# A hybrid decoder step on one core: TensorE in the traced order, the other engines placed by the scheduler

## The chip, the cores and the metric

The kernel runs on one core of one Trainium2 chip. A core has five engines that each work through their own instruction queue: TensorE (PE in the profile, its weight loads shown apart as PEld), VectorE (DVE), ScalarE (ACT), GpSimd (POOL) and SyncE (SP), which here issues the DMAs. The metric is the device time of one execution in microseconds. Before the change the median of three runs was 3425.92 us (3423.82 to 3428.62). A change of under 0.2% (7 us) counts as no difference in what follows.

## What is computed

One layer of a decoder for a prompt of 2048 tokens and for 8 sequences with 8 new tokens each, which have a past of 2048 tokens in pages of keys and values. The reference, cut to what matters:

```python
h = rmsnorm(x, norm_mix) * (1 + sc_m) + sh_m            # sh, sc, g: silu(c) @ w_ada + b_ada
rq, rk, rv, rg, sq, sk, sv = jnp.split(h @ w_in, cuts, axis=-1)
# 4 heads of retention, in chunks of 128 tokens with a running state s
scores = einsum(qc, kc) * decay
o = einsum(scores, vc) + einsum(qc * q_decay, s); s = s * chunk_decay + einsum(kc * k_decay, vc)
ro = groupnorm(o) * ret_gn * silu(rg)
# 8 heads of stick-breaking attention; k, v are the past pages and the new rows
z = q @ k * scale + bias
a = exp(log_sigmoid(z) + reverse_cumsum(log_sigmoid(-z)))    # only keys before the query
so = rmsnorm_per_head(a @ v) * sb_gn
x = x + g_m * (concat([ro, so]) @ w_out)
h = rmsnorm(x, norm_ffn) * (1 + sc_f) + sh_f
x = x + g_f * ((silu(conv3(h @ w_up_gate)) * (h @ w_up_val)) @ w_down)
y = rmsnorm(x, norm_final)
```

## The kernel before

All of it is float32. A dense product is made as three products of values split in a high and a low part: `mm3` (L293) issues them as L295, L296 and L297, so that every weight tile has to be split first, by a cast on ACT (L174) and a subtraction on DVE (L159, the helper through which most tensor operations go). The weight parts are the tiles `whl`, from raw weights `raw` that SP loads; the activations are `act` and `ff`.

The prompt is worked on in four blocks of 512 tokens. The work is written as Python generators, each of which records some instructions and yields a cost: `in_block` (adaLN, input projections; `k_rows` L640 transposes the new keys at L643), `decode` (the 8 sequences against their pages), `ada`, `retention` and `retention_sample`, `attention`, and `mlps` (`out_block` and `ffn_block` for each block of tokens). `_weave` (L138) steps them in turn: it takes the generator whose cost so far is the smallest share of its given total. The order in which the instructions are recorded in this way is the **traced order**. There are three weaves: `in_block`, `decode` and `ada`; then the rest of `in_block` and `ada` with both retentions and the attention of block 0; then `mlps` with the attention of blocks 1 to 3. The last `ffn_block` stands alone.

Three pieces of it matter below, since the change moves them:

- **Attention** (L1122) makes one step for each 128 queries by 512 keys: `turn` of five steps ago (transposes the attention weights, L1173, into a PSUM tile `z`, which ACT and DVE split into the two tiles `ahl`), then `av` of six steps ago (L1185, two matmuls a split, `acc <- ahl, avv`), then `qk` (L1144, two matmuls into a `z`, which ACT turns into `aom` and `abe` at L1147 and L1148, then a scan on DVE). So `av` uses what the `turn` of the step before gave to ACT and DVE.
- **Decode** (L775) makes for each pair of key pages: `k_load` (transposes at L835, which ACT and DVE split into `khl`) and, in the next step, `k_z` (L848, reads `khl`); for the value pages `v_load` (ACT and DVE split the page into `vhl`) and, a step later, `v_mm` (L908, `acc <- vhl, aT`). Pages are loaded into 3 buffers (`page`), `vhl` has 3 buffers, `khl` 2.
- **PSUM** has 4 buffers `d`, 3 buffers `z` and one `acc`; a `z` is free for the next use when ACT or DVE has read it.

After the trace a **scheduler** decides in which order each engine's queue holds its instructions. It plays the program through with estimated durations. Whenever an engine is free in that play, it gets the first instruction in traced order whose inputs and buffers are ready by these estimates; one that isn't ready is passed by. The five queues are then fixed, with the waits on semaphores between them.

## Time and profile before

| | |
|---|---|
| median of 3 runs | 3425.92 us |
| the profiled execution | 3422.1 us |
| its span (first to last instruction) | 3420.4 us |
| mean granted TensorE clock | 0.986 |
| busy DVE, ACT, POOL | 2287.6, 1772.8, 1029.1 us |
| DMA | 527.72 MB, mean 154 GB/s |

A matmul row of the profile has its engine, line, operation, the tiles it writes and reads, the sizes, and its duration; matmuls overlap one another, so a run of 512-column matmuls that the page shows with a mean of 367 to 408 ns each starts one about every 230 ns. "Idle before" is time in which the engine did nothing before an instruction, with the instruction that ended the wait.

### The profile page before, as it was taken

The page shows a single profiled execution, that of the slowest core. Times are in us where ns is not written, and L with a number is a line of the kernel's source. Part 1 is how long each engine was busy: PE and PEld are TensorE (multiplying, and loading weights), DVE is VectorE, ACT ScalarE, POOL GpSimd, SP SyncE. Part 2 cuts the span into 40 slices and gives each one's busy share as a digit, 9 for nine tenths or more (in the row PEclk, how much of TensorE's full clock was granted, in tenths as well). Part 3 has the DMA queues.
Part 4 walks back from the last instruction along what each step waited for, and adds up shares of the span by engine and source line. Part 5 has one row for each costly group of instructions (what it writes and reads, how often), then busy time and mean ns, then how long its engine had stood idle before and what let it go on. Part 6 is the DMA issues. An engine that isn't in the chain of part 4 may idle for free.

```text
span 3420.4 us, 49521 instructions
## 1 busy us (share of the span) xinstructions
PE 3273.5 (96%) x17111; PEld 2676.8 (78%) x17111; DVE 2287.6 (67%) x3258; ACT 1772.8 (52%) x3153; POOL 1029.1 (30%) x1898
## 2 busy tenths in 40 slices
PE   7999999999988989999998999999899999899998
PEld 5877777776777768878877877877788787799997
DVE  5466666764665567777778777877878774554445
ACT  5457556654544446555556555555655553433223
POOL 3012001101443233433344343334433333221113
PEclk9999999999999999999999999999999999999999
DMA  6765776776656773433464343336333334332221
GB/s 235 234 202 191 235 235 209 239 241 206 198 179 193 243 224 95 126 117 113 123 199 122 117 120 108 118 113 197 118 115 108 114 105 146 106 109 81 81 87 66
DMA packets 406233, 527.72 MB, mean 154 GB/s; under 512 B 27830, under 2 KB 244009, under 8 KB 405982
## 3 DMA queue, kind: packets, MB, share of 16 engines
q1 hardware_dynamic: 405982, 524.55, 49.0%
q8 instruction: 136, 2.23, 0.3%
q14 instruction: 115, 0.94, 0.1%
HBM read 442.47 MB, written 81.99 MB: 153 GB/s over the span
## 4 chain that ended last, share of the span: by engine, by line
PE 45%; DVE 2%; POOL 1%; ACT 1%; issue 1%; DMA 1%; SPq 0%; POOLq 0%; DVEq 0%; ACTq 0%
PE d L295 11%; PE d L296 11%; PE d L297 11%; PE acc L1185 3%; PE z L1144 2%; PE z L1173 2%; PE z L297 1%; PE z L296 1%; PE z L295 1%; DVE whl L159 1%; DVE hf L159 1%; DVE aom L1161 0%; POOL ff L159 0%; ACT whl L174 0%; PE z L304 0%
## 5 line engine op out<-in xcount | busy, mean ns | idle before, releaser
L174 ACT CAST whl<-raw 128x1024 fp32r<-128x1024 f32 x456 | 477.2, 1050 | 940.9 <-PE d L296 661.7
L159 DVE TENSOR_TENSOR whl<-raw,whl 128x1024 fp32r<-128x1024 f32 x456 | 573.9, 1262 | 523.1 <-ACT whl L174 514.2
L295 PE MATMUL d<-act,whl 128*128 128x512 f32 (+2 forms) x2016 | 738.8, 367 | 2.3 <-DVE hf L159 1.4
L297 PE MATMUL d<-act,whl 128*128 128x512 f32 (+2 forms) x2016 | 734.3, 364 | 1.1 <-DVE whl L159 1.1
L296 PE MATMUL d<-act,whl 128*128 128x512 f32 (+2 forms) x2016 | 730.9, 363 | 0.2
L295 PEld LDWEIGHTS d<-act,whl 128*128 128x128 f32 x2016 | 382.7, 190 | 62.4 <-issue 3.1
L297 PEld LDWEIGHTS d<-act,whl 128*128 128x128 f32 x2016 | 382.1, 190 | 60.6 <-DVE whl L159 2.2
L296 PEld LDWEIGHTS d<-act,whl 128*128 128x128 f32 x2016 | 383.5, 190 | 55.9 <-issue 0.4
L295 PE MATMUL d<-whl,ff 128*128 128x512 f32 x704 | 279.3, 397 | 0.0
L296 PE MATMUL d<-whl,ff 128*128 128x512 f32 x704 | 278.9, 396 | 0.0
L297 PE MATMUL d<-whl,ff 128*128 128x512 f32 x704 | 278.3, 395 | 0.0
L295 PE MATMUL d<-whl,act 128*128 128x512 f32 x640 | 257.5, 408 | 5.5 <-ACT whl L174 5.5
L296 PE MATMUL d<-whl,act 128*128 128x512 f32 x640 | 258.8, 404 | 0.3 <-DVE whl L159 0.3
L1161 DVE TENSOR_TENSOR_SCAN aom<-aom,acy 128x512 f32<-128x512 f32 x192 | 256.0, 1333 | 3.1 <-ACT aom L1147 2.4
L297 PE MATMUL d<-whl,act 128*128 128x512 f32 x640 | 257.3, 403 | 0.0
L159 DVE TENSOR_TENSOR abe<-abe,aom 128x512 f32<-128x512 f32 (+2 forms) x320 | 230.1, 719 | 29.9 <-POOL abe L1151 7.9
L1185 PE MATMUL acc<-ahl,avv 128*128 128x512 f32 (+3 forms) x640 | 223.5, 411 | 18.4 <-DVE ahl L159 8.4
L1147 ACT ACTIVATE aom<-z,nb 128x512 f32<-128x512 f32 (+2 forms) x320 | 200.9, 628 | 72.6 <-PE z L1144 50.0
L1148 ACT ACTIVATE abe<-z,bb 128x512 f32<-128x512 f32 (+2 forms) x320 | 199.6, 624 | 0.0
L1144 PE MATMUL z<-akk,aq 128*128 128x512 f32 (+3 forms) x640 | 190.5, 375 | 8.6 <-DVE scd L159 5.9
L159 DVE TENSOR_TENSOR ahl<-z,ahl 128x512 fp32r<-128x512 f32 (+1 forms) x320 | 191.3, 598 | 10.3 <-ACT ahl L174 9.9
L1343 DVE SCALAR_TENSOR_TENSOR c<-a,vecs,c 128x512 f32<-128x512 f32 x176 | 133.3, 759 | 81.8 <-ACT c L1340 47.2
(295 smaller groups left out, 6238.9 us busy)
## 6 DMA issues: line engine op xcount, KB each, us to landing
raw<-in_w_in SPq DMA_DIRECT2D x56, 1024.0 KB
raw<-in_w_up_gate SPq DMA_DIRECT2D x44, 1024.0 KB
raw<-in_w_up_val SPq DMA_DIRECT2D x44, 1024.0 KB
akk<-k SPq DMA_DIRECT2D x160, 256.0 KB
page<-in_cache_k_pages SPq DMA_DIRECT2D x128, 256.0 KB
page<-in_cache_v_pages SPq DMA_DIRECT2D x128, 256.0 KB
raw<-in_w_down SPq DMA_DIRECT2D x32, 1024.0 KB
raw<-in_w_ada SPq DMA_DIRECT2D x24, 1024.0 KB
```

The lines of the kernel that those rows point to most:

```text
L159: eng.tensor_tensor(o, a, b, op)
L174: act.copy(hi, src)
L295: pe.matmul(ps, sh, mh, start=start, stop=False)
L296: pe.matmul(ps, sh, ml, start=False, stop=False)
L297: pe.matmul(ps, sl, mh, start=False, stop=stop)
L1144: pe.matmul(z[:, :n], qs[g, h][:, i * P : (i + 1) * P], kk[:, c, :n], start=c == 0, stop=c == 1)
L1147: act.activation(om[:, :n], z[:, :n], AF.Sigmoid, bias=nb[:, h : h + 1], scale=-SCALE)
L1148: act.activation(be[:, :n], z[:, :n], AF.Sigmoid, bias=bb[:, h : h + 1], scale=SCALE)
L1161: dve.tensor_tensor_scan(rv, rv, rv, init, ALU.mult, ALU.bypass)
L1173: pe.transpose(ps[:, i * P : (i + 1) * P], As[u, i][:, kt * P : (kt + 1) * P], ident)
L1185: pe.matmul(accs[0][:, cs], kv[u][1][:, kt, :], m[:, cs], start=(s == g and kt == 0 and c == 0), stop=(s == 0 and kt == NT - 1 and c == 1),)
L1343: dve.scalar_tensor_tensor(c[:, :TB], a[:, j : j + TB], cw(j), c[:, :TB], ALU.mult, ALU.add)
```

## The change

The whole recording now stands in a context that tells the scheduler to leave TensorE's queue as it was traced:

```diff
     with _tile.TileContext(nc) as tc:
-        body(tc, ins, outs)
+        with tc.manual_schedule(engines={mybir.EngineType.PE}):
+            body(tc, ins, outs)
```

No instruction is added or removed. TensorE has 16,670 matmuls and transposes in both. The scheduler still places those of DVE, ACT, POOL and SP, in a play in which TensorE waits at its next instruction in traced order instead of passing it by. Set side by side, the two TensorE queues are equal but for 172 separate stretches, at whose ends the same instructions have been issued; they hold 4,355 instructions. Of the other queues 777 of 3,258 instructions stand elsewhere on DVE, 840 of 3,050 on ACT, 209 of 1,898 on POOL, and 757 of 1,617 on SP; on DVE and ACT by at most 35 places.

The first place is on TensorE, where `decode` begins to compute (185 us into the profiled execution). L835 are transposes of a key page, L848 the scores of `k_z`, L529 a piece of `ada`, L295 to L297 with `d_435` the first projection of the next `in_block` chunk. The queue before:

```order
L835 MATMUL z_407_1939<-con_106_171,page_406_1937 128x128 x4
L295 MATMUL d_435_2081<-act0_114_193,whl_433_2077 128x288
L296 MATMUL d_435_2081<-act0_114_193,whl_433_2077 128x288
L297 MATMUL d_435_2081<-act0_114_193,whl_434_2078 128x288
L295 MATMUL d_435_2081<-act0_114_193,whl_433_2077 128x288
L296 MATMUL d_435_2081<-act0_114_193,whl_433_2077 128x288
L297 MATMUL d_435_2081<-act0_114_193,whl_434_2078 128x288
L848 MATMUL z_408_1946<-khl_403_1907,qbd_402_1901 128x264
```

The queue of the change at the same place (the last number of a name is two higher throughout):

```order
L835 MATMUL z_407_1941<-con_106_173,page_406_1939 128x128 x4
L848 MATMUL z_408_1948<-khl_403_1909,qbd_402_1903 128x264 x8
L835 MATMUL z_415_1983<-con_106_173,page_414_1981 128x128 x4
L835 MATMUL z_417_2001<-con_106_173,page_416_1999 128x128 x4
L529 MATMUL z_420_2011<-whl_421_2012,s18_120_228 18x512
```

The scores `z_408` follow the transposes before them at once; the projection, of which six matmuls stood between them, comes only after two more steps of `decode` and the piece of `ada`.

The second place is on TensorE beside the MLP (1511 us), where two steps of `attention` follow each other without a piece of `mlps` between. `acc_3443` is the attention's output, `ahl_3509` and `ahl_3510` the two halves of one split, `z_3520` the next scores, and `d_3524` to `d_3526` the down projection. The queue before:

```order
L1173 MATMUL z_3516_17903<-con_106_171,abe_3501_17831 128x128
L1185 MATMUL acc_3443_17551<-ahl_3509_17882,avv_3423_17471 128x512
L295 MATMUL d_3524_17929<-whl_3529_17935,ff_3366_17211 128x512
L296 MATMUL d_3524_17929<-whl_3530_17936,ff_3366_17211 128x512
L297 MATMUL d_3524_17929<-whl_3529_17935,ff_3366_17211 128x512
L295 MATMUL d_3525_17930<-whl_3529_17935,ff_3366_17211 128x512
L296 MATMUL d_3525_17930<-whl_3530_17936,ff_3366_17211 128x512
L1144 MATMUL z_3520_17917<-akk_3511_17888,aq_3466_17665 128x512
L1185 MATMUL acc_3443_17551<-ahl_3510_17883,avv_3423_17471 128x512
L1144 MATMUL z_3520_17917<-akk_3511_17888,aq_3466_17665 128x512
```

The queue of the change at the same place:

```order
L1173 MATMUL z_3516_17905<-con_106_173,abe_3501_17833 128x128
L1185 MATMUL acc_3443_17553<-ahl_3509_17884,avv_3423_17473 128x512
L1185 MATMUL acc_3443_17553<-ahl_3510_17885,avv_3423_17473 128x512
L1144 MATMUL z_3520_17919<-akk_3511_17890,aq_3466_17667 128x512 x2
L295 MATMUL d_3524_17931<-whl_3529_17937,ff_3366_17213 128x512
L296 MATMUL d_3524_17931<-whl_3530_17938,ff_3366_17213 128x512
```

The second matmul of `av` and both of `qk` now stand ahead of the five matmuls of the down projection that stood before them.

## The prediction

> **What bounds the kernel now.** I read the page first, then the busy time of each engine by stage.

> ```profile
> span 3420.4 us, 49521 instructions
> PE 3273.5 (96%) x17111; PEld 2676.8 (78%) x17111; DVE 2287.6 (67%) x3258; ACT 1772.8 (52%) x3153; POOL 1029.1 (30%) x1898
> ```

> ```profile
> core 0: us, PE busy (x) PEld busy (x) DVE busy (x) ACT busy (x) POOL busy (x), PEclk, DMA share, GB/s
> 0.00:185.00 185.00, 162.78 (x986) 130.14 (x987) 93.59 (x124) 93.61 (x157) 38.08 (x68) 0.96 0.70 235
> 185.00:815.00 630.00, 602.66 (x3234) 479.00 (x3234) 411.09 (x626) 381.03 (x695) 83.13 (x171) 0.99 0.68 220
> 815.00:1293.00 478.00, 430.85 (x2311) 345.85 (x2312) 280.35 (x578) 224.64 (x458) 176.86 (x372) 0.97 0.66 203
> 1293.00:2870.00 1577.00, 1552.49 (x7414) 1247.35 (x7414) 1230.01 (x1525) 877.16 (x1490) 610.06 (x1040) 1.00 0.41 123
> 2870.00:3421.00 551.00, 524.75 (x3169) 474.46 (x3168) 272.58 (x406) 196.32 (x357) 120.97 (x247) 0.97 0.31 99
> ```

> TensorE is the bound in every stage: 3273.5 of 3420.4 us, idle for 147 us in all. In the longest stage, attention beside the MLP, it is idle for 24 of 1577 us, and no other engine passes 78% there (DVE, 1230 of 1577). So a microsecond in which TensorE stands still is a microsecond of the end, and the change can only move the time by making it wait more or less.

> **The change part by part.** It adds and removes nothing. TensorE's queue differs in 172 stretches. In each, the queue of before passes by an instruction and does other work first; that of the change stops at it. What this costs is read from the trace: when TensorE came to the place, and when ACT, DVE, POOL or a DMA had ended what the passed instruction needs. At the first place that the change section shows:

> ```profile
> 185.29 0.38 PE L295 MATMUL d<-act,whl 128*128 128x288 f32 x1
> 186.44 0.42 DVE L159 TENSOR_TENSOR z<-z,zl 64x264 f32<-64x264 f32 x1
> 186.79 1.27 DVE L159 TENSOR_TENSOR khl<-z,khl 128x512 fp32r<-128x512 f32 x2
> ```

> TensorE was there at 185.29. The scores that now come next need a `z` that DVE reads until 186.86 and the last low half of `khl`, which ends at 188.06. So it would stand for 1.6 us, issue one matmul and stand again for about 1 us. The longest wait of this stage is at a value page:

> ```profile
> 287.60 1.12 PE L848 MATMUL z<-khl,qbd 128*128 128x256 f32 x8
> 293.01 0.60 ACT L174 CAST vhl<-page 128x512 fp32r<-128x512 f32 x1
> ```

> The change has `v_mm` (L908) at 287.60; its cast ends at 293.61, 6 us later. The last place of the stage is small:

> ```profile
> 806.33 0.69 DVE L159 TENSOR_TENSOR vhl<-page,vhl 128x512 fp32r<-128x512 f32 x1 [2.23 <-ACT vhl L174]
> 806.69 0.39 PE L295 MATMUL d<-act,whl 128*128 128x512 f32 x1
> ```

> Its first `v_mm` would start at 807.02 instead of 806.69; with those behind it this place costs 2.9 us.

> I did this for every stretch: its matmuls in the new order, each at the spacing that it has in the trace, none before its inputs' end as traced; what the stretch ends later is its cost. The stage from 185 to 815 has 50 stretches, from the one at 185.29 to that at 806.69, and they cost **106 us**; 60 us of waits are of `v_mm` for a value page.

> Beside the MLP there are 79 stretches, from 1302.88 to 2839.17. The first, the second place of the change section, and the last:

> ```profile
> 1302.88 0.48 PE L295 MATMUL d<-act,whl 128*128 128x512 f32 x1
> 1306.55 0.67 DVE L159 TENSOR_TENSOR o<-acc,sbsq 64x512 f32<-64x512 f32 x1
> ...
> 1511.82 0.39 PE L295 MATMUL d<-whl,ff 128*128 128x512 f32 x1
> 1512.58 0.68 DVE L159 TENSOR_TENSOR ahl<-z,ahl 128x512 fp32r<-128x512 f32 x1
> 1513.36 0.46 PE L1185 MATMUL acc<-ahl,avv 128*128 128x512 f32 x1
> ...
> 2839.17 0.48 PE L295 MATMUL d<-act,whl 128*128 128x512 f32 x1
> 2840.79 0.68 DVE L159 TENSOR_TENSOR ahl<-z,ahl 128x512 fp32r<-128x512 f32 x1
> ```

> At 1302.88 `av` would wait for DVE to read the old `acc` until 1307.22, 4.3 us. At 1511.82 it would wait until 1513.26 for the low half of the split, 1.4 us, while the down projection stands behind it. At 2839.17 the low half ends at 2841.47, 2.3 us. In 64 of the 79 the longest wait is one of `av`; they recur because two attention steps come without a piece of the MLP between. The 79 cost **130 us**.

> The three other stages have one place each here:

> ```profile
> 87.15 0.38 PE L295 MATMUL d<-act,whl 128*128 128x288 f32 x1
> 88.01 0.40 ACT L634 COPY kf<-z 128x288 f32<-128x288 f32 x1
> ...
> 925.93 0.50 PE L295 MATMUL d<-act,whl 128*128 128x512 f32 x1
> 926.23 0.68 ACT L1148 ACTIVATE abe<-z,bb 128x512 f32<-128x512 f32 x1
> ...
> 2956.98 0.40 PE L295 MATMUL d<-whl,ff 128*128 128x512 f32 x1
> 2960.28 1.33 ACT L1293 ACTIVATE c<-ff,rs_b 128x512 f32<-128x512 f32 x2
> ```

> The key transposes wait for a copy that ends at 88.41, 1.3 us; 12 stretches before 185 cost 11 us. The retention's scores wait for ACT to free a `z` at 926.91, 1.0 us; 27 stretches from 815 to 1293 cost 67 us, the long chains of the norms among them. The transposes before the last block's MLP wait for the first of two ACT copies (2960.28 + 0.67), 4 us; four stretches after 2870 cost 7 us. Sum: 11 + 106 + 67 + 130 + 7 = **321 us**.

> What stands behind a waiting matmul is all of TensorE's queue, and behind that, with the same delay, whatever ACT and DVE make of it. Both bounds of the sum lie there. **Above:** I held the producers to their traced times, though most of them start from a TensorE instruction that itself comes later. Timing every producer from the one that feeds it, with the lag that it has in the trace, gives 385 us. **Below:** while TensorE stands, ACT and DVE work off what they have. With nothing queued ahead, the split at 1511.82 is a cast and a subtraction (0.58 and 0.68) after the transposes, against 0.6 of `qk` on TensorE: 0.7 us instead of 1.4. Half the sum, 160 us. I take 321: beside the MLP the queues of DVE and ACT read the same at most of these places before and after, so the same work is queued ahead.

> **The clock** is a second term. Three neighbouring windows of 3.4 us, with TensorE's busy time, its granted clock, the DMA share and GB/s:

> ```profile
> 2419.50:2422.90 3.40, 1.18 (x6) 1.00 0.80 253
> 2422.90:2426.30 3.40, 3.40 (x19) 0.50 0.27 67
> 2426.30:2429.70 3.40, 3.40 (x30) 1.00 0.40 155
> ```

> After a window with TensorE busy for 1.18 us the clock is granted at half for the next, with 19 matmuls instead of 30. So an added wait of some 2 us can halve the next 3.4 us and cost up to 1.7 more. My list holds 59 waits of over 1.9 us; if half of them fall whole within such a window, that is 29 x 1.7 = 50 us at most. Nothing is the other end, since TensorE may be waiting then anyway. I take 30 us, nearer to the row's full price.

> [...]

> Against the profiled execution: 3422.1 + 321 + 30 = 3773. The median of the runs shown is 3.8 us above that execution, so **3777 us**.

> **The rivals.** *The waits melt away.* ACT and DVE, idle for 48% and 33% of the span, get ahead in each wait and the next is shorter. For it speaks the lower bound above; against it that the waits are some 20 us apart beside the MLP, far more than the queue of a wait. It gives 3426 + 160 = 3586.

> *The waits breed.* Chains repeat and the clock falls at most of them: 3426 + 385 + 50 = 3861 and more.

> *Faster.* The queue of before was laid by estimates, and TensorE waits in it, too (us in total, times, longest):

> ```profile
> PE z L835 <- DMA page<-in_cache_k_pages: 5.8, 8, 1.6
> PE z L835 <- issue: 3.1, 1, 3.1
> PE acc L908 <- ACT vhl L174: 6.2, 9, 2.0
> PE acc L908 <- DVE vhl L159: 2.1, 6, 0.7
> PE acc L1185 <- DVE ahl L159: 8.4, 11, 2.3
> PE acc L1185 <- ACT ahl L174: 6.7, 5, 2.5
> ```

> Where a passed instruction was ready on the chip already, or one was pulled ahead and then waited, the traced order loses nothing. By my count 84 us of the idle time lie within the 172 stretches. If they vanished and the new waits came to less than 84 us, the kernel would gain, with half of them left some 42 us: 3384. It decides where the new waits are a quarter of my sum. Against it: 154 of the 172 stretches cost over 0.3 us by the traced times, so the instruction passed by was late on the chip, too.

> *It does nothing*, since other work hides it or the orders come out alike: 3426. The rows of the change section and TensorE's 96% are against it. Nor does a matmul pass a waiting one by itself:

> ```profile
> 1513.03 0.19 PEld L1144 LDWEIGHTS z<-akk,aq 128*128 128x128 f32 x1 [0.32 <-ACT abe L1148]
> 1513.89 0.39 PE L297 MATMUL d<-whl,ff 128*128 128x512 f32 x1
> ```

> L1144 waited for 0.32 us; L297, whose like had been running just before, stood behind it until 1513.89.

> **How the numbers follow.** Forecast, as worked out, 0.75 (its own range 3680 to 3860); melting 0.11 (3480 to 3680); breeding 0.09 (3860 to 4000); faster 0.03; no difference 0.02, where within 0.2% (7 us) is what a measurement cannot tell from no change. The range of 8 in 10 takes the forecast's and the nearer part of melting and breeding: **3600 to 3880**. Faster 0.03, same 0.02, slower 0.95.

> **What would show it.** TensorE's busy time should stay near 3270 while its idle time rises from 147 to some 470 us (the clock adds busy time); the waits of L1185 for `ahl` should grow from some 15 to over 100 us, those of L908 for `vhl` from 8 to some 60; DVE and ACT should keep their busy time. More entries of half clock should appear from 185 to 1293. The prediction is wrong if L1185 does not lead the list of waits, if idle time grows by less than 160 us, or if DVE or ACT near saturation take over the bound.

## The result, and the profile after

| | before | after |
|---|---|---|
| median | 3426.23 us (4 runs) | 3782.63 us (3779.06 to 3783.46, 4 runs) |
| ratio | | 1.1026, 95% interval 1.1012 to 1.104 |
| TensorE idle (span less busy) | 146.9 us | 398.0 us |
| time at half clock | 98.4 us in 17 stretches | 365.4 us in 64 stretches |

Half clock is the time for which the profile shows a granted TensorE clock of 0.5. The changed kernel is 10% slower: 356 us where 351 were forecast. Three of its four executions have a mean granted clock of 0.952 to 0.954; the fourth shows 0.907 although it is the shortest (3779.06 us), and why stays open. The page's head and TensorE's busy time, after:

```profile
span 3781.8 us, 49606 instructions
PE 3383.8 (89%) x17111; PEld 2776.6 (73%) x17111; DVE 2296.9 (61%) x3258; ACT 1777.7 (47%) x3153; POOL 1019.1 (27%) x1898
```

DVE and ACT have worked as long as before (2287.6 and 1772.8 us). TensorE idles for 251 us more, and the same instructions keep it busy for 110 us longer. The busy time by stage of the kernel after, cut where the same TensorE instructions stand as at the stage bounds of the prediction:

```profile
core 0: us, PE busy (x) PEld busy (x) DVE busy (x) ACT busy (x) POOL busy (x), PEclk, DMA share, GB/s
0.00:200.50 200.50, 169.30 (x987) 136.51 (x988) 94.24 (x124) 94.12 (x157) 40.29 (x68) 0.93 0.66 218
200.50:956.80 756.30, 647.26 (x3233) 514.95 (x3233) 418.92 (x631) 385.12 (x699) 85.89 (x171) 0.93 0.58 189
956.80:1505.50 548.70, 450.76 (x2314) 369.13 (x2313) 285.35 (x577) 227.05 (x460) 175.89 (x373) 0.90 0.55 169
1505.50:3224.00 1718.50, 1590.80 (x7415) 1279.91 (x7414) 1227.23 (x1521) 875.20 (x1482) 592.12 (x1039) 0.98 0.38 113
3224.00:3781.80 557.80, 525.63 (x3169) 476.13 (x3167) 271.16 (x406) 196.21 (x357) 124.90 (x247) 0.97 0.30 98
```

Set against the same rows of before (span, and span less TensorE's busy time):

| stage (bounds of before) | waits forecast | longer by | of it idle | of it busy |
|---|---|---|---|---|
| 0 to 185 | 11 | 15.5 | 9.0 | 6.5 |
| 185 to 815, decode | 106 | 126.3 | 81.7 | 44.6 |
| 815 to 1293 | 67 | 70.7 | 50.8 | 19.9 |
| 1293 to 2870, beside the MLP | 130 | 141.5 | 103.2 | 38.3 |
| 2870 to the end | 7 | 7.4 | 6.5 | 0.9 |
| sum | 321 | 361 | 251 | 110 |

The granted clock (PEclk) has fallen in every stage but the last, most from 185 to 1293: from 0.99 and 0.97 to 0.93 and 0.90. TensorE's longest waits after (us in total, times, longest):

```profile
PE acc L1185 <- DVE ahl L159: 58.8, 62, 2.0
PE acc L1185 <- ACT ahl L174: 22.9, 20, 4.6
PE acc L908 <- ACT vhl L174: 19.8, 11, 4.3
PE acc L1185 <- DVE o L159: 18.3, 6, 4.1
PE d L295 <- DVE hf L159: 14.0, 3, 6.4
PE acc L908 <- DVE vhl L159: 13.9, 13, 2.6
PE z L835 <- DVE z L159: 13.8, 13, 3.0
PE z L1144 <- DVE scd L159: 13.7, 8, 2.6
PE z L1144 <- DMA akk<-k: 13.5, 1, 13.5
```

L1185 leads, with 81.7 us for `ahl` (15.1 before); L908 waits for `vhl` for 33.7 us (8.3 before). Three of the places worked out in the prediction, in the timeline after: the first scores of decode (185.29 of before), the first `av` of the third weave (1302.88), and the down projection (1511.82):

```profile
202.43 0.36 PE L848 MATMUL z<-khl,qbd 128*128 128x264 f32 x1 [1.47 <-DVE z L159]
203.63 1.88 PE L848 MATMUL z<-khl,qbd 128*128 128x264 f32 x7 [0.83 <-DVE khl L159]
...
1519.63 0.73 PE L1185 MATMUL acc<-ahl,avv 128*128 128x512 f32 x2 [4.12 <-DVE o L159]
...
1749.26 0.50 PE L1185 MATMUL acc<-ahl,avv 128*128 128x512 f32 x1 [1.34 <-DVE ahl L159]
```

Forecast were 1.6 and about 1 us, 4.3, and 1.4; measured, 1.47 and 0.83, 4.12, and 1.34. The place at 287.60 went otherwise, and it shows the clock as well:

```profile
341.92 0.73 PE L908 MATMUL acc<-vhl,aT 128*128 128x512 f32 x2
342.49 1.12 PE L848 MATMUL z<-khl,qbd 128*128 128x256 f32 x8
343.45 0.60 PE L835 MATMUL z<-con,page 128*128 128x128 f32 x4
347.04 1.11 PE L835 MATMUL z<-con,page 128*128 128x128 f32 x4 [3.00 <-DVE z L159]
347.81 1.20 PE L908 MATMUL acc<-vhl,aT 128*128 128x512 f32 x2
348.81 0.63 PE L295 MATMUL d<-whl,act 128*128 128x512 f32 x1
349.24 0.63 PE L296 MATMUL d<-whl,act 128*128 128x512 f32 x1
349.66 0.46 PE L297 MATMUL d<-whl,act 128*128 128x512 f32 x1
349.96 0.40 PE L295 MATMUL d<-whl,act 128*128 128x512 f32 x1
350.20 0.39 PE L296 MATMUL d<-whl,act 128*128 128x512 f32 x1
```

The `v_mm` for which 6 us of waiting were forecast is issued at 341.92 without any; the next key page's transposes then wait 3.00 us for a `z`. After that pause the matmuls start 0.43 us apart, and from 349.96 on 0.23 to 0.24. The windows around it, TensorE's busy time first, the granted clock behind POOL:

```profile
342.97:346.39 3.42, 1.08 (x10) 0.84 (x8) 0.00 (x0) 2.79 (x8) 1.11 (x4) 1.00 0.28 77
346.39:349.80 3.41, 2.76 (x9) 2.37 (x10) 1.50 (x3) 3.17 (x7) 0.77 (x3) 0.50 0.06 19
349.80:353.21 3.41, 3.41 (x16) 2.75 (x15) 3.41 (x6) 2.49 (x4) 0.37 (x2) 1.00 0.31 72
```

### The profile page after: what moved, and what is told of

The parts are those of the page before. It is cut to its first block, busy times and chain, and to the rows that moved or that the text cites. A ratio compares the mean times of both kernels' runs of the same rounds, so it can differ in the third digit from the quotient of the medians.

```text
span 3781.8 us, 49606 instructions
## 1 busy us (share of the span) xinstructions
PE 3383.8 (89%) x17111; PEld 2776.6 (73%) x17111; DVE 2296.9 (61%) x3258; ACT 1777.7 (47%) x3153; POOL 1019.1 (27%) x1898
## 3 DMA queue, kind: packets, MB, share of 16 engines
q8 instruction: 136, 2.23, 0.2%
## 4 chain that ended last, share of the span: by engine, by line
PE 69%; DVE 11%; ACT 8%; issue 5%; POOL 4%; DMA 3%; SPq 0%; POOLq 0%; ACTq 0%; DVEq 0%
PE d L295 17%; PE d L296 17%; PE d L297 16%; DVE whl L159 4%; ACT whl L174 3%; PE z L1144 3%; PE acc L1185 2%; PE z L1173 2%; PE z L297 2%; PE z L295 2%; PE z L296 2%; DVE ahl L159 1%; PE acc L908 1%; POOL rs_b L159 1%; DMA page<-in_cache_v_pages 1%
## 5 line engine op out<-in xcount | busy, mean ns | idle before, releaser
L174 ACT CAST whl<-raw 128x1024 fp32r<-128x1024 f32 x456 | 478.0, 1050 | 1207.6 <-PE d L296 929.8
L159 DVE TENSOR_TENSOR whl<-raw,whl 128x1024 fp32r<-128x1024 f32 x456 | 578.6, 1271 | 751.8 <-ACT whl L174 730.7
L295 PE MATMUL d<-act,whl 128*128 128x512 f32 (+2 forms) x2016 | 753.7, 374 | 14.0 <-DVE hf L159 14.0
L297 PE MATMUL d<-act,whl 128*128 128x512 f32 (+2 forms) x2016 | 743.5, 369 | 0.1
L296 PE MATMUL d<-act,whl 128*128 128x512 f32 (+2 forms) x2016 | 742.3, 368 | 0.0
L295 PEld LDWEIGHTS d<-act,whl 128*128 128x128 f32 x2016 | 393.7, 195 | 77.8 <-DVE hf L159 8.0
L296 PEld LDWEIGHTS d<-act,whl 128*128 128x128 f32 x2016 | 394.1, 195 | 60.8 <-DVE act L159 0.2
L297 PEld LDWEIGHTS d<-act,whl 128*128 128x128 f32 x2016 | 391.3, 194 | 64.2 <-DVE whl L159 0.3
L1185 PE MATMUL acc<-ahl,avv 128*128 128x512 f32 (+3 forms) x640 | 228.2, 422 | 102.4 <-DVE ahl L159 58.8
L295 PE MATMUL d<-whl,ff 128*128 128x512 f32 x704 | 281.4, 400 | 0.0
L297 PE MATMUL d<-whl,ff 128*128 128x512 f32 x704 | 279.4, 397 | 0.0
L295 PE MATMUL d<-whl,act 128*128 128x512 f32 x640 | 264.6, 413 | 6.5 <-ACT whl L174 6.5
L296 PE MATMUL d<-whl,act 128*128 128x512 f32 x640 | 260.8, 407 | 0.5 <-DVE whl L159 0.5
L297 PE MATMUL d<-whl,act 128*128 128x512 f32 x640 | 260.1, 406 | 0.0
L159 DVE TENSOR_TENSOR abe<-abe,aom 128x512 f32<-128x512 f32 (+2 forms) x320 | 231.1, 722 | 29.3 <-POOL abe L1151 7.0
L1144 PE MATMUL z<-akk,aq 128*128 128x512 f32 (+3 forms) x640 | 188.2, 377 | 32.5 <-DVE scd L159 13.7
L1185 PEld LDWEIGHTS acc<-ahl,avv 128*128 128x128 f32 x640 | 103.0, 193 | 132.1 <-DVE ahl L159 76.7
L1148 ACT ACTIVATE abe<-z,bb 128x512 f32<-128x512 f32 (+2 forms) x320 | 199.6, 624 | 0.0
L159 DVE TENSOR_TENSOR ahl<-z,ahl 128x512 fp32r<-128x512 f32 (+1 forms) x320 | 191.1, 597 | 6.8 <-ACT ahl L174 6.5
```

Source lines behind the costliest of these rows:

```text
L159: eng.tensor_tensor(o, a, b, op)
L174: act.copy(hi, src)
L295: pe.matmul(ps, sh, mh, start=start, stop=False)
L296: pe.matmul(ps, sh, ml, start=False, stop=False)
L297: pe.matmul(ps, sl, mh, start=False, stop=stop)
L1144: pe.matmul(z[:, :n], qs[g, h][:, i * P : (i + 1) * P], kk[:, c, :n], start=c == 0, stop=c == 1)
```

## The experiments

All kernels are measured beside the kernel before on the same chip. Where an edit adds lines above it, the profile's line numbers move: L1185 is then L1198, L643 is L656 and so on.

### The traced order in one weave alone

The context stands around one `_weave` call and not around the whole:

```diff
-            _weave([ins, side, rest], side)
+            with tc.manual_schedule(engines={mybir.EngineType.PE}):
+                _weave([ins, side, rest], side)
```

and likewise around the second and the third.

First weave: 

> Only the first weave (input projections, decode, ada) keeps TensorE's traced order; everything else is placed as before. Theory of local waits (each stage's growth comes from its own traced order): this stage alone grew by 126.9 us between common points of the two traces, so 3426 + 127 = 3553 us (3535 to 3570), with TensorE's idle time up by about 82 us and its busy time by about 45, both before the second weave begins. Rival, carry-over (what one stage shifts, the next pays or saves): off that by 30 us or more, with the stages behind the first weave longer or shorter than before by as much.

Second weave: 

> Only the second weave (rest of the projections, both retentions, attention of block 0) keeps the traced order. Local waits: 3426 + 70 = 3496 us (3480 to 3512), TensorE idle up by about 51 us. The 13.5 us wait of L1144 for the keys' DMA, if it belongs to this order, comes again here. Carry-over: under 3460 or over 3530.

Third weave: 

> Only the third weave (MLP blocks 0 to 2 beside attention of blocks 1 to 3) keeps the traced order. Local waits: 3426 + 142 = 3568 us (3550 to 3585), TensorE idle up by about 103 us, L1185 heading the waits with 80 us or more. Carry-over: off by 30 us or more. With the two kernels before: if the three growths add up to 361 less the 23 us of the head and the tail (some 338), the stages don't feed on one another.

Measured: 3571.74 us (ratio 1.0423, 1.04 to 1.0446), 3470.60 us (1.0132, 1.0108 to 1.0156) and 3592.86 us (1.048, 1.0458 to 1.0503), against 3427.67. The growths are 144, 43 and 165 us, 352 in sum of the 356 of the whole change. Each single number missed its forecast by 19 to 25 us and lies outside its stated range, the first and the third weave too long and the second too short. The reason is where I had cut: the stage bound at 815 us lies before the end of decode, and that at 1293 us in the third weave, not between two. Cut where a weave's own last instructions start (L918 ends decode, L989 the retention, L1185 the attention), rows of before and then of after:

```profile
L918 PE MATMUL z<-con,tm x64: 170/256/361, 359.5 to 833.3; 128*128 128x8 f32 x64
L989 PE MATMUL z<-con,on x68: 222/272/333, 925.5 to 1220.7; 128*128 128x128 f32 x64, 64*128 64x64 f32 x4
L1185 PE MATMUL acc<-ahl,avv x640: 222/398/796, 919.6 to 2858.6; 128*128 128x512 f32 x128, 128*128 128x256 f32 x32
```

```profile
L918 PE MATMUL z<-con,tm x64: 172/256/383, 425.2 to 972.2; 128*128 128x8 f32 x64
L989 PE MATMUL z<-con,on x68: 223/273/474, 1081.2 to 1408.3; 128*128 128x128 f32 x64, 64*128 64x64 f32 x4
L1185 PE MATMUL acc<-ahl,avv x640: 272/399/795, 1067.8 to 3205.7; 128*128 128x512 f32 x128, 128*128 128x256 f32 x32
```

From the last start in each row (973.0, 1365.6 and 3002.6 in the first kernel, 835.8, 1266.4 and 2903.2 in the second, 835.6, 1224.6 and 3017.7 in the third), the growth over before in us:

| traced order in | to L918 | to L989 | to L1185 | to the end |
|---|---|---|---|---|
| everything (after) | 138.9 | 48.7 | 159.5 | 14.3 |
| first weave | **139.7** | 5.2 | -0.9 | 3.3 |
| second weave | 2.5 | **43.2** | -1.1 | 1.8 |
| third weave | 2.3 | 1.6 | **155.2** | 11.4 |

So hardly anything is carried over: each weave pays for its own order what it pays in the whole change, within 6 us. The waits neither breed nor melt from one weave to the next; within a weave this says nothing.

### Multiplications by zero in the waits

```diff
+        for _ in range(0 if first else plan.get(k, 0)):
+            pe.matmul(acc, zero.to_broadcast([P, P]), zero.to_broadcast([P, 512]), start=False, stop=False)
```

stands ahead of the matmuls of L908 and L1185 that waited in the trace after; `plan` holds their numbers and counts.

> The changed kernel with multiplications by zero put into TensorE's queue ahead of the 109 matmuls of L1185 and L908 that waited 0.4 us or more in its trace, as many of 512 columns as fit into each wait (at most 10), 101 us in all; they add zero to the accumulator, so the result stays. Theory that TensorE's own pauses lower its clock: TensorE's idle time falls from 398 to about 310 us, half-clock time falls from 365 us towards 265, and since these waits are 101 of 251 us of added idle, 40% of the 110 us of added busy time of real work goes: 3783 - 44 = 3739 us (3720 to 3765). Rival, the clock falls for another reason (the kind of work, or the chip's load): half-clock time stays at 340 us or more, and the time at 3783 or above, by what doesn't fit into the waits (up to 3810).

Measured: 3768.18 us (3764.22 to 3776.51), 14 less than the changed kernel. Its page and waits:

```profile
PE 3441.3 (91%) x17476; PEld 2818.9 (75%) x17476; DVE 2295.8 (61%) x3259; ACT 1778.9 (47%) x3153; POOL 1023.4 (27%) x1898
```

```profile
PE acc L1198 <- DVE ahl L170: 17.4, 63, 0.6
```

```profile
L163 PE MATMUL acc<-zero x365: 377/381/463, 418.3 to 3168.3; 128*128 128x512 f32 x183
```

The edit put in less than the expectation says. `plan` holds 432 multiplications, but seven of its entries, with 67 of them, are first matmuls of an accumulation, and `first` leaves those out; so the 18.2 us for `o` stay. The 365 others added some 80 us to TensorE's busy time, not 101. The span was 3763.5 us, so TensorE's idle time is 322 us and not 398 (of the 58.8 us for `ahl` after DVE 17.4 are left), and half clock fell from 365.4 us in 64 stretches to 307 in 51. More work in TensorE's queue made the kernel no slower, and its half clock fell as the theory of the pauses has it, though not to the 265 us expected; the rival's 340 us of half clock are out. The time alone is a weaker sign: the executions lie apart (3764 to 3777 against 3779 to 3783), but the 95% intervals of the two ratios overlap (1.0972 to 1.1028 and 1.1012 to 1.104). The gain is a third of the 44 us expected. The two traces show where it went: idle time fell by 76 us, which the multiplications' 80 used up, and the busy time of the real work fell by 22 us. If TensorE were busy all through the 58 us less of half clock and took twice its time there, they would be worth 29, an estimate.

### A longer distance by the step

`av` two steps behind its transposes, in blocks 1 to 3:

```diff
...
+            if lag == 7 <= t < total + lag:
+                av(*divmod(t - lag, 4))
             if 5 <= t < total + 5:
                 turn(*divmod(t - 5, 4))
-            if 6 <= t < total + 6:
-                av(*divmod(t - 6, 4))
+            if lag == 6 <= t < total + lag:
+                av(*divmod(t - lag, 4))
```

> The changed kernel with TensorE in traced order, but the trace itself changed: in the attention of blocks 1 to 3 the two matmuls of L1185 follow the transposes of their keys by two steps, not by one (and stand ahead of the step's transposes, so that the six buffers of ahl are enough). Theory that the growth beside the MLP is the time between a producer on ACT or DVE and its reader on TensorE: the 81.7 us of waits of L1185 for ahl fall under 30, with them some 25 us of half-clock loss: 3783 - 80 = 3703 us (3680 to 3725). Rival, the next wait takes its place (transposes wait for abe or for a z to come free): L1173 and L1144 wait for as much more, 3770 to 3795.

`v_mm` two steps behind `v_load` (`v_mm(*vs[nv - 2])`, `v_out` a step later):

> The changed kernel, with the value pages' matmuls of L908 two steps behind their splits and not one. Theory of the short distance: the 33.7 us that L908 waited for vhl fall under 10, and 10 us of half-clock loss go: 3783 - 34 = 3749 us (3735 to 3765). Rival, the page loads or the z buffers set this stage: 3775 or more, with L835 waiting longer.

`k_z` two steps behind `k_load` (`k_z(*ks[t - 2])`):

> The changed kernel, with the scores of the key pages (L848) two steps behind their splits and not one, in the same two buffers of khl. Theory of the short distance: the 16.7 us that L848 waited for khl go, and 7 us of half-clock loss: 3760 us (3745 to 3775). Rival, the two buffers: each split now has to wait until the scores of two steps ago have read the buffer, the z buffers stay full for longer, and L835 waits for z by more than L848 gains: 3785 to 3830.

All three in the kernel before, with the scheduler:

> The kernel before (TensorE placed by the scheduler) with all three of these longer distances in the trace. Theory that the scheduler already passes by what isn't ready: little is left to gain, the 15.1 us of waits of L1185 for ahl and 8.3 of L908 for vhl at most: 3415 us (3400 to 3430). Rival, the longer distances keep buffers for longer and the scheduler loses by it: 3435 or more.

Measured: 3739.43 us (`av`), 3809.77 (`v_mm`), 3772.67 (`k_z`), where the changed kernel has 3782.63; and 3439.33 us for all three with the scheduler, a ratio of 1.0044 (1.003 to 1.0058). The groups of the first, then waits of the second:

```profile
L1144 PE MATMUL z<-akk,aq 128*128 128x512 f32 (+3 forms) x640 | 210.5, 411 | 94.7 <-ACT abe L1148 36.9 <-DVE ahl L159 28.3 <-DVE scd L159 13.7
...
L1185 PE MATMUL acc<-ahl,avv 128*128 128x512 f32 (+3 forms) x640 | 186.4, 373 | 17.9 <-ACT aom L1147 9.0
```

```profile
PE z L835 <- DMA page<-in_cache_k_pages: 27.8, 11, 7.4
PE acc L908 <- ACT vhl L174: 17.0, 10, 4.7
PE acc L908 <- DVE vhl L159: 8.3, 10, 2.2
```

The waits of L1185 did go, from 102.4 us of idle before it to 17.9, but L1144, which needs neither `ahl` nor `abe`, now waits 65 us until those two have been made, that is until a `z` is free: transposes and scores stand back to back and there are three `z`. Both theories hold in part, and the gain is 43 us where 80 were expected; the time lies in neither's range. The edit also moved `av` ahead of the transposes, and no run separates that from the longer distance. With `v_mm` later, L908 waits 25 us instead of 34, and L835 waits 27.8 us for key pages (5.5 after): the rival holds, 27 us slower. With `k_z` later the median is 10 us lower where 23 were expected, which isn't clear of the noise (ratio 1.0993 to 1.103 against 1.1012 to 1.104); L848 waits 2.4 us for `khl` instead of 16.7, and L835 waits 20.0 us for pages there. A step more of distance in the same buffers mostly moves the wait. The scheduler has nothing to gain from it; it loses 15 us, as its rival had it.

### A longer distance by finer interleaving

Here the trace, not the lag, is changed. After each triple L295 to L297 the generator that records it lets another one record a piece, if that one is behind its share, and the steps are cut into pieces. In the attention:

```diff
+    def pump(cost):
+        main, sides = beside
+        main.part += cost
+        for s in sorted((s for s in sides if s.live), key=lambda s: s.got / s.total):
+            if s.got / s.total >= (main.got + main.part) / main.total or s.step():
+                return
...
                 turn(*divmod(t - 5, 4))
-            if 6 <= t < total + 6:
-                av(*divmod(t - 6, 4))
+            yield 0.4
...
                 qk(*divmod(t, 4))
+            yield 0.4
+            if 5 <= t < total + 5:
+                av(*divmod(t - 5, 4))
...
-            yield 1.3
+            yield 0.5
```

In decode, `k_at`, `k_z` and `k_load` get a `yield` each.

Third weave, traced order there only: 

> TensorE in traced order in the third weave only, as in the kernel that measured 3593 us, but that trace is interleaved more finely: after each triple of matmuls (L295 to L297) the attention may record one piece, and its step is three pieces (transposes, then scores, then L1185 on this step's own ahl), so that some four triples, about 3 us of TensorE's work, stand between the transposes and their L1185, with the lags and buffers otherwise as they were or shorter. Theory of distance (a wait is the producer's time less TensorE's work in between): the 102 us of waits of L1185 fall under 25, half-clock time with them, 3593 - 130 = 3463 us (3440 to 3495). Rival, the waits come from a backlog on DVE and ACT in this stage or from the three z buffers: they reappear at L1144 and L1173, 3540 us or more.

First weave, traced order there only: 

> The same fine interleave in the first weave, TensorE in traced order there only (3572 us without the interleave): decode and ada may record a piece after each triple of the projections, and a step of the key pages is three pieces. Theory of distance: of 82 us of added idle time two thirds go, and half of the 45 us of added busy time: 3572 - 80 = 3492 us (3465 to 3525). Rival, the pages' transfers or their three buffers set this stage: 3550 or more, with L835 waiting for its pages.

All three weaves, TensorE placed by the scheduler: 

> The fine interleave in all three weaves, with TensorE placed by the scheduler as in the kernel before. Theory that the scheduler makes up for a coarse trace: it finds the same work ready, 3427 +- 12 us. Rival, it places by the trace where several are ready, and a finer trace leaves TensorE fewer waits (147 us idle before): 3380 to 3414.

Measured: 3467.28 us (ratio 1.0123, 1.0104 to 1.0142), 3534.81 us (1.032, 1.0302 to 1.0338) and 3432.72 us (1.0017, 1.0003 to 1.0031). The group of `av` with the coarse and then the fine trace, and the costliest wait left in the first weave:

```profile
L1185 PE MATMUL acc<-ahl,avv 128*128 128x512 f32 (+3 forms) x640 | 228.4, 421 | 105.0 <-DVE ahl L159 58.8 <-ACT ahl L174 24.7 <-DVE o L159 18.2
```

```profile
L1198 PE MATMUL acc<-ahl,avv 128*128 128x512 f32 (+3 forms) x640 | 196.2, 376 | 30.5 <-DVE ahl L161 22.6 <-ACT ahl L176 5.5 <-ACT on L992 1.3
```

```profile
PE z L656 <- ACT kf L647: 35.0, 16, 3.7
```

In the third weave 126 of the 165 us are gone, as expected, although `av` now reads the `ahl` of its own step: with four triples between, the split is mostly done in time (30.5 us of idle time are left before `av`, where under 25 were expected), and the scores wait for a `z` almost nowhere (the group of L1157, the former L1144, below: nearly all of its idle time is the load of keys). The scores also moved ahead of `av` within the step; no run separates that from the finer interleaving.

```profile
L1157 PE MATMUL z<-akk,aq 128*128 128x512 f32 (+3 forms) x640 | 182.8, 367 | 20.8 <-DMA akk<-k 20.5 <-DVE hf L161 0.2
```

In the first weave 37 us went, half of what was expected, and the time lies outside the stated range, though below the rival's: the new keys' transposes read a copy recorded right ahead of them, and that wait grew to 35 us, from 10 in the kernel without the interleave. The scheduler makes next to nothing out of the finer trace (ratio 1.0017, as its first theory had it). A last kernel has the change's traced order throughout, the fine interleave in all weaves, and those transposes four triples later:

> The whole of TensorE's queue in traced order, as in the change, with the fine interleave in all three weaves, and the new keys' transposes (L643 of the changed kernel) recorded four triples after the copy kf that they read, since they were the longest wait of the finely interleaved first weave (35.0 us). If the gains found one by one add up: 3783 less 126 (third weave), less 37 (first weave), less some 30 (the transposes, with their share of half clock) = 3590 us (3560 to 3625); some 10 us of that for the second weave if it gains too. What stays against 3427 is the head and the tail (23 us) and waits for page loads and z buffers. Rival, the stages feed on one another or the finer trace holds the z buffers for longer: 3640 or more.

Measured: 3568.78 us (ratio 1.0417, 1.0391 to 1.0442), 214 us better than the changed kernel and within the forecast range. It is 21 below the forecast sum, in which the 30 for the transposes were an estimate and the second weave counted nothing; their wait for `kf` fell from 35.0 to 9.0 us.

```profile
PE 3304.2 (93%) x17111; PEld 2723.9 (76%) x17111; DVE 2312.2 (65%) x3258; ACT 1799.5 (50%) x3153; POOL 1035.1 (29%) x1898
```

With a span of 3567.9 us, idle time is 264 us, and 31 us of added busy time stay. No kernel tried here beats the one before.

## Why the prediction was right

- **The bound.** TensorE stayed it, and DVE and ACT kept their busy time. That its idle and busy time add up to the span is so by definition; what bears the argument out is where the time grew. The stages were right: 35, 20 and 39% of the growth lie in the three large ones (126.3, 70.7 and 141.5 us), where 33, 21 and 40% of the sum of waits had been put (106, 67 and 130).
- **The sum of waits** was mis-sized: 321 forecast, 251 measured as added idle time, 76 to 79% of the forecast in each of the three large stages. Part of the gap lies in the measure. The forecast counted how much later TensorE gets on, but a wait doesn't show wholly as idle time: the first matmul after a pause overlaps no other, and in the trace of after it adds 0.23 us more to the busy time than its like in a run (61.3 us over the 263 at full clock). After has 333 pauses, before 192. By this estimate 33 us of waiting stand in the busy time, and some 284 us came of the 321; beside the MLP, with 66 pauses more, some 120 of 130. Places with a short chain came as worked out (4.12 for 4.3, 1.34 for 1.4). In decode it was the chains through pages that were off, 33.7 us of L908 for `vhl` where some 60 were named, and at 287.60 none: the step that failed there is the choice between the sum's bounds, with the producers held to their traced times. In the retention's stage it stays open which chains fell short.
- **The clock** was mis-sized the other way: 30 us taken, 50 the upper end, 110 measured as added busy time of the same instructions. Not all of the 110 is the clock. With the 33 us of the pauses taken off, and 20 us put back by which matmuls in runs at full clock took less in sum than their likes before, some 97 are left, an estimate again. It fits the records of the clock: in half clock TensorE was busy for 289 us, 72 before, and if work took twice its time there (the starts in the timeline of after lie 0.43 us apart, and 0.23 to 0.24 behind it, a little less than twice) the difference would cost 108, which is the most. The step that failed is the counting of single waits over 1.9 us. Of the 64 stretches of half clock, 27 follow a window of 3.41 us into which no wait of 1.8 us or more reaches. In 11 of these windows shorter waits add up to 1.8 us or more; the other 16 held less idle time, and what lowered the clock behind them stays open. Busy time, which was to stay near 3270 but for what the clock adds, rose to 3384.
- **The total** was right because errors cancel, and that is luck: 70 us too much and 80 too little as idle and busy time show it. By the estimates above the waits were put 37 us too high and the clock 67 too low, and the runs at full clock, whose 20 us less were not forecast, make up for part of it. TensorE at half clock may have left its producers more time, and the one error so have fed the other; no run here shows that.
- **What would show it.** L1185 leads the waits with 81.7 us for `ahl`, where over 100 were named, and 102.4 with those for `o`. Idle time grew by 251, above the 160 at which the argument would have fallen and below the 323 forecast. Half clock came where it was put: 39 of the 64 stretches lie in the two stages from 185 to 1293, 9 of 17 before.
- **Unforeseen** was the single longest wait, 13.5 us for the first keys of the third weave. Before, the scheduler had put MLP work ahead of their scores, which followed the weave's first MLP matmuls by 24 us; in traced order TensorE comes to them after 7 (1429.10 less 13.51) and stands until the keys have landed. With traced order in the third weave alone the wait was 21.2 us, so it belongs to that weave's order. The timeline of before, then of after:

```profile
1221.23 0.47 PE L295 MATMUL d<-whl,act 128*128 128x512 f32 x1
...
1244.95 0.97 PE L1144 MATMUL z<-akk,aq 128*128 128x128 f32 x6
```

```profile
1408.40 0.77 PE L295 MATMUL d<-whl,act 128*128 128x512 f32 x1
...
1429.10 1.19 PE L1144 MATMUL z<-akk,aq 128*128 128x128 f32 x4 [13.51 <-DMA akk<-k]
```

- **The rivals.** Melting and breeding both need one wait to change the next; by the table of the single weaves they hardly touch one another. Within a stage, melting is there at most to the extent of what is missing from the sum of waits, some 37 us by the estimate above.

## What to carry to other kernels

The traced order cost TensorE here what its producers took, less the work that the trace put between (in the third weave 126 of 165 us went with some four triples put there); before handing an engine's order over to the trace, measure that distance for each pair of producer and reader, and buy it with finer interleaving of independent work rather than with a longer lag in the same buffers (here 43 us gained, 27 lost, and 10 gained that aren't clear of the noise). With a scheduler that passes by what isn't ready the trace's order mattered little here (1.0017 with the fine trace, 1.0044 with the longer distances), so a fine trace paid only where the order was fixed. When adding up many small waits of TensorE, add them per window first (here of 3.413 us, the grid on which half clock began): the clock was more than a quarter of the whole (some 97 of 361 us).
